# Attention scores: sorted dilated queries, and the low key parts of two heads in one tile

## The chip, the cores and the metric

The kernel runs on one core of one Trainium2 chip. The metric is the device time of one execution in microseconds (us). The profile is one execution, recorded instruction by instruction; its span runs from the first to the last instruction.

## The reference, cut to what matters

The program is a two-layer decoder trunk over 1024 tokens of width 1024. Layer 0 has a gMLP mixer beside an attention mixer, layer 1 a gated linear attention; each is followed by a gated MLP with a short convolution. The change touches layer 0's mixer alone:

```python
B_HEADS, B_HEAD_DIM, B_BLOCK = 8, 64, 128
B_BRANCHES = ((128, 1), (512, 4), (2048, 16))       # window, dilation

qh = rms_norm(heads(q), q_g); kh = rms_norm(heads(k), k_g); vh = heads(vb)
for window, dilation in B_BRANCHES:
    # query t attends to t, t-d, ..., t-window; positions m*d + r form residue
    # subsequences, each a causal band in blocks of 128 (this block and the one before)
    s = jnp.einsum('bhrnic,bhrnjc->bhrnij', qb, kk) * (hd ** -0.5)
    s = jnp.where(valid, s, NEG)
    m = jnp.max(s, -1, keepdims=True); p = jnp.exp(s - m); den = jnp.sum(p, -1)
    o = jnp.einsum('bhrnij,bhrnjc->bhrnic', p, vv) / den[..., None]
    lse = m[..., 0] + jnp.log(den)
wts = jax.nn.softmax(jnp.stack(lses), axis=0)        # over the three branches
o = jnp.einsum('rbhs,rbhsc->bhsc', wts, jnp.stack(outs))
```

## The kernel before

**Precision.** Queries and keys are held as two parts, a high part rounded to fp32r and a low part, the rest (`split`). A score is then (high + low) of the query times (high + low) of the key.

**Work and loops.** The eight heads are done as four pairs (`p` = 0 to 3). `project(p)` goes over eight tiles of 128 tokens (`n`). For each it multiplies the token tile with the pair's weights (`pj`, 24 matmuls of 128x384, in `mm_tok`, L190), normalises (`qn`; row sums on DVE, the power on POOL), puts the parts side by side (`qs`, `ks`), transposes them on TensorE (`tq`, L707; `tk`, L713) and copies them to `qT` and `kT`. It then runs one local block through `unit`. After the eight tiles, `dilated(p)` runs eight blocks of dilation 4; the branch of dilation 16 falls within them and is met by the mask `mboth`. `combine` joins the two sets of outputs.

**The operands of the scores.** `qT` holds, for each head, 64 rows of high part above 64 rows of low part, tokens in order; a dilated block takes its 128 queries as every fourth column. `kT` holds four parts, for each head the high part twice (128 rows) and the low part twice, with the tokens sorted by residue of 4. So one head's score is two matmuls of 128 rows into one PSUM tile `sc`, one with the doubled high key part and one with the doubled low (`scores`, L638).

**After the scores.** DVE adds the mask and takes the row minimum of the negated scores in one instruction (L643), ACT takes the exponential (L644), TensorE transposes the weights (`pP`, L658), DVE or ACT in turn copies them (`pT`, L663 and L661), and TensorE multiplies them with the values (`po`, L666).

**gMLP.** `gmlp` and `u_proj` project to `pv` and `pu`; for each half of the tokens eight products `pm` (L581), one for each group, go to PSUM and DVE adds the bias (L582).

**Order and buffers.** The program is written in its natural order; a scheduler that simulates the engines' time then orders the instructions on each engine. So the projection of pair p+1 stands among the dilated blocks of pair p, and the gMLP among those of the last. Each engine runs its own list in order. PSUM has eight banks, given out by tag: `pt` 2, `sc` 2, `pj` 2, `po` 1, `tq` 1. The `sc` tag serves the scores (one tile for each head of a block) and `pm`.

Of the kernel before, what the change touches and what calls it, by code (L numbers as in the profile page):

```python
# [9 lines left out]
F32 = mybir.dt.float32  # L10
# [45 lines left out]
def trunk(ctx: ExitStack, tc: tile.TileContext, a, out):  # L56
# [452 lines left out]
    def even(gm_open):  # L509
        with ExitStack() as st:  # L510
            pools = {}
            for tag, bufs in (("pt", 2), ("sc", 2), ("pj", 2), ("po", 1), ("tq", 1)):
                pools[tag] = st.enter_context(tc.tile_pool(name="ps_" + tag, bufs=bufs, space=PSUM, reuse_waits="tile"))
            ps = Tagged(pools)
            pq = st.enter_context(tc.tile_pool(name="pq", bufs=1, reuse_waits="tile"))
            par0 = ExitStack()
            pq0 = par0.enter_context(tc.tile_pool(name="pq0", bufs=1, side="right", reuse_waits="tile"))
            with tc.tile_pool(name="nrm", bufs=1, reuse_waits="tile") as pool:
                for n in range(NT):
                    xt = pool.tile([P, D], F32, tag="x", bufs=3, name=f"x0{n}")  # L520
                    Q.dma_start(xt, rows(a["x"], n))
                    if n == 0:
                        Q.dma_start(g0, a["norm_mix_gT"])
                    for g in range(2):
                        pt = ps.tile([P, 4, P], F32, tag="pt", name=f"pt{n}{g}")
                        for j in range(4):
                            k = 2 * j + g
                            T.transpose(pt[:, j, :], xt[:, k * P : (k + 1) * P], ident)
                        split(place(hq[g][n // 4], n), pt)
                    if n == 1:  # L530
                        wq0 = load_qkv(0)
                    h = pool.tile([P, D], F32, tag="h", bufs=2, name=f"h{n}")
                    ssq = small.tile([P, 1], F32, tag="ssq", name=f"ssq{n}")
                    A.activation(h, xt, AF.Square, accum_out=ssq)
                    inv_rms(ssq, 1, D, f"rn{n}", r0[:, n : n + 1])
            with tc.tile_pool(name="at", bufs=2, reuse_waits="tile") as at, \
                    tc.tile_pool(name="av", bufs=1, reuse_waits="tile") as av:
                return attention(ps, at, av, pq, pq0, par0, wq0, gm_open)
# [11 lines left out]
    def gmlp(ps, gm):  # L550
# [14 lines left out]
        def consume(n, pj):  # L565
            gv = gm.tile([P, 512], F32, tag="gv", bufs=2, name=f"gv{n}")
            A.activation(gv, pj, AF.Gelu, scale=r0[:, n : n + 1])
            st = small.tile([P, 6], F32, tag="bn", name=f"bn{n}")
            V.bn_stats(st, gv)
            mv = small.tile([P, 2], F32, tag="mv", name=f"mv{n}")  # L570
            V.bn_aggr(mv, st)
            r = inv_rms(mv[:, 1:2], 1, 1, f"lr{n}")
            V.tensor_scalar(gv, gv, mv[:, 0:1], r, op0=ALU.subtract, op1=ALU.mult)
            V.tensor_mul(gv, gv, lnG)
            half, j = n // 4, n % 4
            V.tensor_add(mx[half][:, j, :], gv, lnB)
            if j == 3:
                for g in range(GROUPS):
                    gc = mx[half][:, :, g * 64 : g * 64 + 64]
                    pm = ps.tile([P, 4, 64], F32, tag="sc", name=f"pm{half}{g}")  # L580
                    T.matmul(pm, ws[:, g, :], gc, start=True, stop=True)  # L581
                    V.tensor_scalar(gc, pm, bs[:, g : g + 1], None, op0=ALU.add)  # L582

# [13 lines left out]
    def attention(ps, at, av, pq, pq0, par0, wq0, gm_open):  # L597
# [33 lines left out]

            return t.rearrange("p s (m r) -> p s r m", r=4)

        def scores(p, name, q, k, W, mask, nm, den, wide):

            sc = ps.tile([P, 256], F32, tag="sc", name="sc" + name)
            for i in range(2):
                T.matmul(sc[:, :W], q, k(i), start=(i == 0), stop=(i == 1))  # L638
            sm = at.tile([P, 256], F32, tag="sm", name="sm" + name, bufs=3)[:, :W]
            o, c, m = wide(sm), sc[:, :W], wide(mask)  # L640
            if len(o.shape) > 2:
                c = c.rearrange("p (r m) -> p r m", r=4)
            V.tensor_tensor_reduce(out=o, in0=c, in1=m, scale=1.0, scalar=3e38, op0=ALU.add, op1=ALU.min, accum_out=nm)  # L643
# [3 lines left out]
        def unit(p, name, i, ot, po, qv, kv, vb, mask, wide=lambda t: t):  # L647
# [2 lines left out]
            nj = len(vb)  # L650
            W = nj * P
            pts = ps.tile([P, 2, nj, P], F32, tag="pt", name="pP" + name)
            for s in range(2):
                sm = scores(p, f"{name}{s}", qv(s), lambda part: kv(s, part), W,
                            mask[:, 2 * P - W :],
                            ot[:, i, 128 + s : 129 + s], ot[:, i, 130 + s : 131 + s], wide)
                for j in range(nj):
                    T.transpose(pts[:, s, j, :], sm[:, j * P : j * P + P], ident)  # L658
# [14 lines left out]
        def project(p, ws=None, then=None):  # L673
# [2 lines left out]
            ws = ws or load_qkv(p)  # L676
            pool = pq if p % 2 else pq0
            qT = pool.tile([P, 2, S], F32R, tag="qT", bufs=1, name=f"qT{p}")
            kT = pool.tile([P, 4, S], F32R, tag="kT", bufs=1, name=f"kT{p}")
            vd = dram.tile([S, P], F32, name=f"vd{p}")  # L680
            vN, os = [], []
            for n in range(NT):
# [14 lines left out]
                A.mul(vN[n], pj[:, 256:384], rn)  # L697
                Q.dma_start(rows(vd, n), vN[n])
                qs = pq.tile([P, 2, P], F32R, tag="qs", bufs=2, name=f"qs{p}{n}")
                ks = pq.tile([P, 4, P], F32R, tag="ks", bufs=2, name=f"ks{p}{n}")  # L700
                split([qs[:, :, :64], qs[:, :, 64:]], heads(qn[:, :P]), hi=G.tensor_copy)
                kk = ks.rearrange("p (h i) (x c) -> p h i x c", i=2, x=2)
                split([kk[:, :, i] for i in range(2)], heads(qn[:, P:])[:, :, None, :].to_broadcast([P, 2, 2, 64]),
                      hi=G.tensor_copy)
                tq = ps.tile([P, 2, P], F32R, tag="tq", name=f"tq{p}{n}")
                for j in range(2):
                    T.transpose(tq[:, j, :], qs[:, j, :], identr)  # L707
                ts_ = slice(n * P, n * P + P)
                A.copy(qT[:, :, ts_], f32(tq))
                four = lambda t: t.rearrange("p s (r m) -> p s r m", r=4)[:, :, :, 32 * n : 32 * n + 32]  # L710
                tk = ps.tile([P, 4, P], F32R, tag="tq", name=f"tk{p}{n}")
                for j in range(4):
                    T.transpose(tk[:, j, :], ks[:, j, :], identr)  # L713
                (V.tensor_copy if n % 2 else A.copy)(four(kT), by4(f32(tk)))

                if n % 4 == 0:
# [1 line left out]
                    os.append(ot)  # L718
                m0 = max(n - 1, 0)
                unit(p, f"{p}n{n}", n % 4, ot, po, lambda s: qT[:, s, ts_],  # L720
                     lambda s, i: kT[:, 2 * s + i, :].rearrange("p (r m) -> p r m", r=4)[:, :, 32 * m0 : 32 * n + 32],
                     vN[m0 : n + 1], mband, lambda t: t.rearrange("p (m r) -> p r m", r=4))
                if n % 4 == 3:
                    A.copy(ot[:, :, :P], po)
# [2 lines left out]
            v4 = av.tile([P, 4, 2, P], F32, tag="v4", name=f"v4{p}", bufs=1)  # L727
            for b in range(2):
                Q.dma_start(v4[:, :, b, :], vd.rearrange("(b m r) c -> b m r c", b=2, r=4)[b])
            return os, qT, kT, v4  # L730

        def dilated(p, qT, kT, v4):

            od = dram.tile([S, 132], F32, name=f"od{p}")
            for g in range(2):
                ot, po = outputs(f"{p}d{g}")
                for i in range(4):
                    r, b = 2 * g + i // 2, i % 2
# [507 lines left out]
```

## Time and profile before

| | |
|---|---|
| Median of three timed executions | 2200.07 us (2199.83 to 2200.43) |
| Span of the profiled execution | 2191.9 us (its own time is not listed apart from the span) |
| Mean granted TensorE clock | 0.998 |
| Busy, share of span | TensorE 98%, weight loads 83%, DVE 70%, ACT 48%, POOL 21% |
| Matmuls | 10508 |
| First and last score matmul (L638) | 37.8 and 353.8 us after the span's start |
| First and last `pm` product (L581) | 357.0 and 394.7 us |

In the profile's rows, PE is TensorE's matmuls and PEld its weight loads; a row of the timeline gives the start, the length, the engine, the line of the code, the tiles written and read, the count of merged instructions, and in brackets the idle time before it with what ended it. A row of groups gives busy time, the mean of one in ns, and the idle time before with its releasers. Matmuls overlap one another, so the length of a merged row holds the tail of its last one.

### The profile page before, as it was taken

How to read it: one execution, taken by the hardware profiler on the slowest of the kernel's cores; microseconds unless marked ns; L12 is line 12 of the kernel's file. 1: busy time of each engine (PE TensorE's matmuls, PEld its weight loads, DVE VectorE, ACT ScalarE, POOL GpSimd, SP SyncE). 2: the span in 40 equal slices, each digit the busy share in tenths (PEclk: the TensorE clock that was granted, in tenths of full speed). 3: DMA queues.
4: the chain of work that ended last, by engine and by line, in shares of the span. 5: the costliest groups of instructions: out<-in, count | busy, mean ns of one | idle time of the engine just before them, and what ended most of it. 6: DMA issues, size and time to landing. Idle time of an engine off the chain costs nothing.

```text
span 2191.9 us, 29865 instructions
## 1 busy us (share of the span) xinstructions
PE 2154.9 (98%) x10508; PEld 1826.3 (83%) x10508; DVE 1532.8 (70%) x2459; ACT 1045.2 (48%) x2006; POOL 468.6 (21%) x487
## 2 busy tenths in 40 slices
PE   8999999999999999999999999999999999999999
PEld 7999987877888888878889787878888888888887
DVE  5566555457888797855577777666887888885554
ACT  6455565246444444444453555534644444454443
POOL 3333320003334252200010011110232424320000
PEclk9999999999999999999999999999999999999999
DMA  4122212565444444575563232378544444557555
GB/s 141 49 77 80 66 48 63 175 242 194 163 158 156 153 158 159 185 287 181 203 234 122 67 98 96 106 234 287 203 150 151 158 166 155 168 177 269 203 195 203
DMA packets 157254, 349.59 MB, mean 159 GB/s; under 512 B 17408, under 2 KB 54272, under 8 KB 156720
## 3 DMA queue, kind: packets, MB, share of 16 engines
q1 hardware_dynamic: 157104, 347.68, 46.9%
q8 instruction: 83, 1.36, 0.3%
q14 instruction: 67, 0.55, 0.1%
HBM read 239.02 MB, written 108.59 MB: 159 GB/s over the span
## 4 chain that ended last, share of the span: by engine, by line
PE 85%; DMA 4%; DVE 4%; ACT 3%; issue 3%; POOL 1%; SPq 0%; ACTq 0%; DVEq 0%; POOLq 0%
PE pgB L290 11%; PE puB L290 11%; PE pgC L290 5%; PE puC L290 5%; PE pj L190 5%; PE pv L190 5%; PE pdB L397 5%; PE pdC L397 5%; PE po L190 5%; PE pdO L397 4%; PE puA L290 3%; PE pgA L290 3%; PE pdP L397 2%; PE pdQ L397 2%; PE pBq L958 2%
## 5 line engine op out<-in xcount | busy, mean ns | idle before, releaser
L101 DVE TENSOR_TENSOR da<-ar,da 128x512 fp32r<-128x512 f32 x154 | 106.2, 690 | 154.3 <-ACT da L100 154.1
L100 ACT CAST da<-ar 128x512 fp32r<-128x512 f32 x154 | 95.9, 623 | 208.3 <-PE pdC L397 89.2
L190 PE MATMUL po<-wo,hq 128*128 128x512 f32 x768 | 184.0, 394 | 1.3 <-ACT hq L100 0.9
L190 PEld LDWEIGHTS po<-wo,hq 128*128 128x128 f32 x768 | 141.7, 188 | 31.2 <-ACT hq L100 1.3
L190 PE MATMUL pj<-wq,hq 128*128 128x384 f32 x768 | 154.4, 347 | 1.5 <-ACT wq L105 1.0
L190 PE MATMUL pv<-wv,hq 128*128 128x512 f32 (+2 forms) x768 | 141.1, 340 | 2.5 <-DVE b L990 1.6
L397 PE MATMUL pdB<-dw,da 128*128 128x512 f32 x528 | 136.2, 391 | 0.8 <-ACT dw L100 0.8
L397 PE MATMUL pdC<-dw,da 128*128 128x512 f32 x528 | 135.8, 390 | 0.0
L190 PEld LDWEIGHTS pj<-wq,hq 128*128 128x128 f32 x768 | 133.3, 191 | 2.7 <-ACT wq L105 1.4
L190 PEld LDWEIGHTS pv<-wv,hq 128*128 128x128 f32 x768 | 118.8, 189 | 17.5 <-DVE b L990 2.1
L397 PEld LDWEIGHTS pdB<-dw,da 128*128 128x128 f32 x528 | 98.7, 188 | 22.1 <-ACT dw L100 1.3
L397 PEld LDWEIGHTS pdC<-dw,da 128*128 128x128 f32 x528 | 99.1, 188 | 20.4
L101 DVE TENSOR_TENSOR dw<-wr,dw 128x512 fp32r<-128x512 f32 x154 | 105.8, 687 | 12.1 <-ACT dw L100 11.8
L256 POOL TENSOR_TENSOR S1g<-rg 128x512 f32<-128x512 f32 x20 | 30.7, 1536 | 381.2 <-DMA wsd<-D 302.0
L140 POOL TENSOR_SCALAR rn<-ssq 128x1 f32<-128x1 f32 x24 | 8.7, 364 | 471.4 <-ACT h L148 245.5
L100 ACT CAST dw<-wr 128x512 fp32r<-128x512 f32 x154 | 95.0, 617 | 15.9 <-DMA wr<-in_w_dn 6.3
L397 PE MATMUL pdO<-dw,da 128*128 128x512 f32 x396 | 102.2, 389 | 0.1
L397 PEld LDWEIGHTS pdO<-dw,da 128*128 128x128 f32 x396 | 74.3, 188 | 15.9 <-DVE dw L101 0.6
L319 DVE SCALAR_TENSOR_TENSOR t<-g,cw,t 128x1022 f32<-128x1022 f32 x44 | 76.6, 1742 | 0.1
L318 DVE SCALAR_TENSOR_TENSOR t<-g,cw,t 128x1023 f32<-128x1023 f32 x44 | 59.3, 1349 | 16.5 <-ACT t L317 16.5
L303 DVE TENSOR_TENSOR g<-g,s1g 128x512 f32<-128x512 f32 x22 | 16.2, 737 | 77.0 <-ACT s1g L302 77.0
L320 ACT ACTIVATE t<-t 128x1024 f32<-128x1024 f32 x44 | 46.7, 1061 | 31.4 <-DVE t L319 31.4
(1069 smaller groups left out, 5407.5 us busy)
## 6 DMA issues: line engine op xcount, KB each, us to landing
ar<-actd SPq DMA_DIRECT2D x70, 512.0 KB, 3.5
rd<-in_w_down SPq DMA_DIRECT2D x44, 512.0 KB, 3.6
wsd<-D SPq DMA_DIRECT2D x88, 256.0 KB, 2.5
rg<-in_w_gate SPq DMA_DIRECT2D x42, 512.0 KB, 3.6
ru<-in_w_up SPq DMA_DIRECT2D x42, 512.0 KB, 4.6
wr<-wsd SPq DMA_DIRECT2D x40, 512.0 KB, 4.6
actd<-t SPq DMA_DIRECT2D x66, 256.0 KB, 2.2
wr<-in_w_dn SPq DMA_DIRECT2D x30, 512.0 KB, 4.8
```

What stands on the lines that cost most here:

```text
L100: (hi or A.copy)(dst[0], src)
L101: (lo or V.tensor_sub)(dst[1], src, f32(dst[0]))
L140: G.tensor_scalar(r, ssq, 1.0 / n, EPS, op0=ALU.mult, op1=ALU.add)
L190: T.matmul(o, L[i], R[jj][:, sl], start=(k == 0 and (ii, jj) == PASSES[0]), stop=(k == nk - 1 and (ii, jj) == PASSES[-1]))
L256: G.tensor_tensor(sums[name], x, y, op=op)
L290: T.matmul(o, L[ii][:, j * P : j * P + P], right[p][:, jj, j, :], skip_group_check=more, start=(not more and j == 0 and (ii, jj) == PASSES ...
L303: V.tensor_add(C22, C22, s1)
L318: V.scalar_tensor_tensor(t[:, 1:], g[:, : S - 1], w(1), t[:, 1:], op0=ALU.mult, op1=ALU.add)
L319: V.scalar_tensor_tensor(t[:, 2:], g[:, : S - 2], w(0), t[:, 2:], op0=ALU.mult, op1=ALU.add)
L320: A.activation(t, t, AF.Silu)
L397: T.matmul(o, L[ii][:, t * P : t * P + P], R[jj], skip_group_check=more, start=start and not more and (ii, jj) == PASSES[0], stop=stop and ...
L958: T.matmul(o, L[ii][:, j * P : j * P + P], right[p][:, jj, j, :], skip_group_check=more, start=(not more and j == 0 and (ii, jj) == PASSES ...
```

## The change

- The low part of the keys is held once for each head: `ks` has three parts, the first head's doubled high part, the second head's doubled high part, and both heads' low parts side by side. `tk` has three transposes instead of four, `kT` three parts.
- `qs` of the second head has its low part above its high part, so that the high query parts of the two heads lie in rows 0 to 63 and 64 to 127, as the low key parts do.
- A head's score is one matmul of 128 rows with the doubled high key part (high and low query times high key), and one of 64 rows (high query times low key). The product of the two low parts is left out.
- Both heads of a block have their scores in one tile of two banks, `[P, 2, 512]`; the tag `sc` has one such buffer instead of two of one bank. The four matmuls are issued first, then each head's mask, minimum and exponential. `pm` takes a tile of the same shape and uses its first bank.
- POOL copies each token tile of `qT` into a new tile `qR` sorted by residue of 4; dilated blocks read their queries there, as 128 columns that lie together.
- The scratch for dynamic DMA is 1024 bytes.

```diff
@@ -577,7 +577,7 @@
             if j == 3:
                 for g in range(GROUPS):
                     gc = mx[half][:, :, g * 64 : g * 64 + 64]
-                    pm = ps.tile([P, 4, 64], F32, tag="sc", name=f"pm{half}{g}")
+                    pm = ps.tile([P, 2, 512], F32, tag="sc", name=f"pm{half}{g}")[:, 0, :256].rearrange("p (a b) -> p a b", a=4)
                     T.matmul(pm, ws[:, g, :], gc, start=True, stop=True)
                     V.tensor_scalar(gc, pm, bs[:, g : g + 1], None, op0=ALU.add)
 
@@ -631,13 +631,11 @@
 
             return t.rearrange("p s (m r) -> p s r m", r=4)
 
-        def scores(p, name, q, k, W, mask, nm, den, wide):
-
-            sc = ps.tile([P, 256], F32, tag="sc", name="sc" + name)
-            for i in range(2):
-                T.matmul(sc[:, :W], q, k(i), start=(i == 0), stop=(i == 1))
+        def scores(name, sc, mask, nm, den, wide):
+
+            W = sc.shape[-1]
             sm = at.tile([P, 256], F32, tag="sm", name="sm" + name, bufs=3)[:, :W]
-            o, c, m = wide(sm), sc[:, :W], wide(mask)
+            o, c, m = wide(sm), sc, wide(mask)
             if len(o.shape) > 2:
                 c = c.rearrange("p (r m) -> p r m", r=4)
             V.tensor_tensor_reduce(out=o, in0=c, in1=m, scale=1.0, scalar=3e38, op0=ALU.add, op1=ALU.min, accum_out=nm)
@@ -650,9 +648,15 @@
             nj = len(vb)
             W = nj * P
             pts = ps.tile([P, 2, nj, P], F32, tag="pt", name="pP" + name)
+            both = ps.tile([P, 2, 512], F32, tag="sc", name=f"sc{name}")
+            scs = [both[:, s, :W] for s in range(2)]
             for s in range(2):
-                sm = scores(p, f"{name}{s}", qv(s), lambda part: kv(s, part), W,
-                            mask[:, 2 * P - W :],
+                T.matmul(scs[s], qv(s), kv(s), start=True, stop=False)
+            for s in range(2):
+                half = slice(64 * s, 64 * s + 64)
+                T.matmul(scs[s], qv(s)[half], kv(2)[half], start=False, stop=True)
+            for s in range(2):
+                sm = scores(f"{name}{s}", scs[s], mask[:, 2 * P - W :],
                             ot[:, i, 128 + s : 129 + s], ot[:, i, 130 + s : 131 + s], wide)
                 for j in range(nj):
                     T.transpose(pts[:, s, j, :], sm[:, j * P : j * P + P], ident)
@@ -676,7 +680,8 @@
             ws = ws or load_qkv(p)
             pool = pq if p % 2 else pq0
             qT = pool.tile([P, 2, S], F32R, tag="qT", bufs=1, name=f"qT{p}")
-            kT = pool.tile([P, 4, S], F32R, tag="kT", bufs=1, name=f"kT{p}")
+            qR = pool.tile([P, 2, S], F32R, tag="qR", bufs=1, name=f"qR{p}")
+            kT = pool.tile([P, 3, S], F32R, tag="kT", bufs=1, name=f"kT{p}")
             vd = dram.tile([S, P], F32, name=f"vd{p}")
             vN, os = [], []
             for n in range(NT):
@@ -697,19 +702,21 @@
                 A.mul(vN[n], pj[:, 256:384], rn)
                 Q.dma_start(rows(vd, n), vN[n])
                 qs = pq.tile([P, 2, P], F32R, tag="qs", bufs=2, name=f"qs{p}{n}")
-                ks = pq.tile([P, 4, P], F32R, tag="ks", bufs=2, name=f"ks{p}{n}")
-                split([qs[:, :, :64], qs[:, :, 64:]], heads(qn[:, :P]), hi=G.tensor_copy)
-                kk = ks.rearrange("p (h i) (x c) -> p h i x c", i=2, x=2)
-                split([kk[:, :, i] for i in range(2)], heads(qn[:, P:])[:, :, None, :].to_broadcast([P, 2, 2, 64]),
-                      hi=G.tensor_copy)
+                ks = pq.tile([P, 3, P], F32R, tag="ks", bufs=2, name=f"ks{p}{n}")
+                q4 = qs.rearrange("p h (x c) -> p (h x) c", c=64)
+                split([q4[:, ::3], q4[:, 1:3]], heads(qn[:, :P]), hi=G.tensor_copy)
+                kh = ks[:, :2].rearrange("p h (x c) -> p h x c", c=64)
+                G.tensor_copy(kh, heads(qn[:, P:])[:, :, None, :].to_broadcast([P, 2, 2, 64]))
+                V.tensor_sub(heads(ks[:, 2]), heads(qn[:, P:]), f32(kh[:, :, 0]))
                 tq = ps.tile([P, 2, P], F32R, tag="tq", name=f"tq{p}{n}")
                 for j in range(2):
                     T.transpose(tq[:, j, :], qs[:, j, :], identr)
                 ts_ = slice(n * P, n * P + P)
                 A.copy(qT[:, :, ts_], f32(tq))
                 four = lambda t: t.rearrange("p s (r m) -> p s r m", r=4)[:, :, :, 32 * n : 32 * n + 32]
-                tk = ps.tile([P, 4, P], F32R, tag="tq", name=f"tk{p}{n}")
-                for j in range(4):
+                G.tensor_copy(four(qR), by4(f32(qT[:, :, ts_])))
+                tk = ps.tile([P, 3, P], F32R, tag="tq", name=f"tk{p}{n}")
+                for j in range(3):
                     T.transpose(tk[:, j, :], ks[:, j, :], identr)
                 (V.tensor_copy if n % 2 else A.copy)(four(kT), by4(f32(tk)))
 
@@ -718,7 +725,7 @@
                     os.append(ot)
                 m0 = max(n - 1, 0)
                 unit(p, f"{p}n{n}", n % 4, ot, po, lambda s: qT[:, s, ts_],
-                     lambda s, i: kT[:, 2 * s + i, :].rearrange("p (r m) -> p r m", r=4)[:, :, 32 * m0 : 32 * n + 32],
+                     lambda s: kT[:, s, :].rearrange("p (r m) -> p r m", r=4)[:, :, 32 * m0 : 32 * n + 32],
                      vN[m0 : n + 1], mband, lambda t: t.rearrange("p (m r) -> p r m", r=4))
                 if n % 4 == 3:
                     A.copy(ot[:, :, :P], po)
@@ -727,9 +734,9 @@
             v4 = av.tile([P, 4, 2, P], F32, tag="v4", name=f"v4{p}", bufs=1)
             for b in range(2):
                 Q.dma_start(v4[:, :, b, :], vd.rearrange("(b m r) c -> b m r c", b=2, r=4)[b])
-            return os, qT, kT, v4
-
-        def dilated(p, qT, kT, v4):
+            return os, qR, kT, v4
+
+        def dilated(p, qR, kT, v4):
 
             od = dram.tile([S, 132], F32, name=f"od{p}")
             for g in range(2):
@@ -737,8 +744,8 @@
                 for i in range(4):
                     r, b = 2 * g + i // 2, i % 2
                     at0 = r * 256
-                    unit(p, f"{p}d{g}{i}", i, ot, po, lambda s: qT[:, s, b * 512 + r : b * 512 + 512 : 4],
-                         lambda s, part: kT[:, 2 * s + part, at0 : at0 + b * P + P],
+                    unit(p, f"{p}d{g}{i}", i, ot, po, lambda s: qR[:, s, at0 + b * P : at0 + b * P + P],
+                         lambda s: kT[:, s, at0 : at0 + b * P + P],
                          [v4[:, r, j, :] for j in range(b + 1)], mboth)
                 A.copy(ot[:, :, :P], po)
                 for b in range(2):
@@ -1235,7 +1242,7 @@
     import concourse.bacc as bacc
     from concourse.bass_utils import run_bass_kernel_spmd
 
-    nc = bacc.Bacc("TRN2", target_bir_lowering=False, num_devices=1)
+    nc = bacc.Bacc("TRN2", target_bir_lowering=False, num_devices=1, dynamic_dma_scratch_size=1024)
     arrays = layouts(inputs)
     aps = {n: nc.dram_tensor("in_" + n, v.shape, F32, kind="ExternalInput").ap() for n, v in arrays.items()}
     out = nc.dram_tensor("out", (S, D), F32, kind="ExternalOutput").ap()
```

(In `even`, the pool of the tag `sc` goes from `("sc", 2)` to `("sc", 1)`.)

More of the change, by code (lines that the diff above doesn't have):

```diff
@@ L511, in even @@
             pools = {}
-            for tag, bufs in (("pt", 2), ("sc", 2), ("pj", 2), ("po", 1), ("tq", 1)):
+            for tag, bufs in (("pt", 2), ("sc", 1), ("pj", 2), ("po", 1), ("tq", 1)):
                 pools[tag] = st.enter_context(tc.tile_pool(name="ps_" + tag, bufs=bufs, space=PSUM, reuse_waits="tile"))
```

## The prediction

> **What bounds the kernel now.** The page comes first: the engines' busy time and the chain that ended last.
>
> ```profile
> span 2191.9 us, 29865 instructions
> PE 2154.9 (98%) x10508; PEld 1826.3 (83%) x10508; DVE 1532.8 (70%) x2459; ACT 1045.2 (48%) x2006; POOL 468.6 (21%) x487
> PE 85%; DMA 4%; DVE 4%; ACT 3%; issue 3%; POOL 1%; SPq 0%; ACTq 0%; DVEq 0%; POOLq 0%
> ```
>
> TensorE carries 85% of the chain. A matmul's modelled time overlaps its neighbour's, so 98% busy only says that gaps are few; what a matmul costs is read from one start to the next. The windows are next: an ordinary attention stretch, the junction of two pairs, and the end of attention.
>
> ```profile
> 150.00:200.00 50.00, 49.79 (x348) 48.84 (x346) 27.09 (x103) 27.09 (x87) 12.48 (x22) 1.00 0.16 45
> 355.00:402.00 47.00, 42.56 (x197) 34.61 (x197) 19.29 (x49) 13.00 (x21) 3.04 (x2) 1.00 0.25 77
> 180.00:193.00 13.00, 12.79 (x105) 12.09 (x105) 9.36 (x36) 10.24 (x35) 2.10 (x4) 1.00 0.31 80
> ```
>
> The columns after the length are PE, PEld, DVE, ACT, POOL, granted clock, DMA share, GB/s. From 150 to 200 TensorE stands for 0.2 of 50 us: attention is bound by TensorE's issue, and what is saved there is saved from the end. At the junction (180 to 193) ACT is busy 10.24 of 13 us, which will matter. Then the tile view of the score matmuls, local (sc1n) and dilated (sc1d):
>
> ```profile
> L638 PEld LDWEIGHTS sc1n<-kT,qT x32: 186/188/216, 114.2 to 152.6; 128*128 128x128 f32 x32
> L638 PE MATMUL sc1n<-kT,qT x32: 277/283/388, 114.3 to 152.7; 128*128 128x256 f32 x28, 128*128 128x128 f32 x4
> L638 PEld LDWEIGHTS sc1d<-kT,qT x32: 307/329/333, 154.6 to 181.8; 128*128 128x128 f32 x32
> L638 PE MATMUL sc1d<-kT,qT x32: 278/399/483, 154.8 to 181.9; 128*128 128x128 f32 x16, 128*128 128x256 f32 x16
> ```
>
> Same shape, but the dilated weight load, whose queries lie four elements apart, takes 329 ns against 188. The timeline says what this costs in issue:
>
> ```profile
> 181.16 1.19 PE L638 MATMUL sc1d<-kT,qT 128*128 128x256 f32 x4
> 182.19 0.29 PE L707 MATMUL tq<-identr,qs 128*128 128x128 f32 x2
> ...
> 183.23 0.30 PEld L638 LDWEIGHTS sc2n<-kT,qT 128*128 128x128 f32 x2
> 183.48 0.14 PEld L658 LDWEIGHTS pP1d<-ident,sm1d 128*128 128x128 f32 x1
> 183.79 0.40 PEld L713 LDWEIGHTS tk<-identr,ks 128*128 128x128 f32 x4
> 184.13 0.42 PEld L658 LDWEIGHTS pP1d<-ident,sm1d 128*128 128x128 f32 x4
> ...
> 213.29 0.64 PE L638 MATMUL sc2n<-kT,qT 128*128 128x256 f32 x4
> 213.76 0.28 PE L707 MATMUL tq<-identr,qs 128*128 128x128 f32 x2
> ...
> 232.39 1.01 PEld L638 LDWEIGHTS sc2d<-kT,qT 128*128 128x128 f32 x4
> 233.34 0.20 PEld L658 LDWEIGHTS pP2d<-ident,sm2d 128*128 128x128 f32 x2
> ```
>
> From the first of a group to the next instruction, over the count: dilated, 256 wide, 1.03/4 = 0.258 us; local, 256 wide, 0.47/4 = 0.118; dilated, 128 wide, 0.95/4 = 0.238; local, 128 wide, 0.25/2 = 0.125; a transpose of ks 0.34/4 = 0.085.
>
> **Part 1: sorted queries (removes).** There are 128 dilated score matmuls (four pairs of 32), half of each width, and all then load contiguous queries: 64 x (0.258 - 0.118) + 64 x (0.238 - 0.125) = 9.0 + 7.2 = 16.2 us less on TensorE.
>
> **Part 2: three key parts instead of four (removes).** 32 transposes go: 32 x 0.085 = 2.7 us. DVE's low part halves and the kT copies shrink by a quarter; both engines have slack outside the junctions, so nothing is counted.
>
> **Part 3: the sorted copy (adds on POOL).**
>
> ```profile
> L100 POOL CAST ks<-qn 128x256 fp32r<-128x256 f32 x29 | 13.1, 450 | 0.9 <-PE tk L713 0.9
> L140 POOL TENSOR_SCALAR rq<-ss 128x4 f32<-128x4 f32 x28 | 8.5, 304 | 86.9 <-DVE ss L691 86.6
> L101 DVE TENSOR_TENSOR ks<-qn,ks 128x256 fp32r<-128x256 f32 x31 | 12.9, 417 | 0.0
> ```
>
> 32 copies of 256 elements at about 0.45 us are 14 us of POOL, which now waits 86.6 us for the row sums alone. The copy waits for ACT's qT; queued behind it in POOL's order are the next token tile's rq and qn, for which DVE and then the transposes wait. The projection runs two PSUM buffers ahead, 24 matmuls each, and covers that: zero. Without that cover, 32 x 0.45 = 14 us. That ks now waits for its high half on POOL alone is the same wait as before. No DMA is added, and none was issued from POOL whose scratch shrinks: zero.
>
> **Part 4: matmuls of 64 rows (changes).** In the changed program's order a block's scores are high, high, low, low, the low ones on rows 0 to 63 and 64 to 127 into two banks. No matmul of the trace has 64 rows, so this is bounded. Below: the two run as one and save 64 x 0.118 = 7.5 us. Above: each change between 128 and 64 rows waits for the matmul before it to end (0.283 modelled, less 0.118 spacing = 0.165) and then for a load that nothing covers (0.118): 0.28 us, at 132 changes in the order (some groups are split) 37 us. I take 0.14 a change, the nearest row being the dilated load, where TensorE likewise waits for a load that isn't covered (0.258 against 0.118): 132 x 0.14 = 18.5; a quarter of the blocks stand where TensorE will wait anyway (part 5), so 13.9; less 7.5 for the pairs: +6.4 us.
>
> [...]
>
> **Part 5: one score tile instead of two (adds a wait).** Before, a head's scores waited for the same head's reduction of the block before; now all four matmuls wait for both reductions.
>
> ```profile
> 182.03 0.42 DVE L643 CUSTOM_DVE_ANT_0 sm1d<-sc1d,mboth 128x256 f32<-128x256 f32 x1 [0.57 <-PE sc1d L638]
> 184.17 0.62 PE L658 MATMUL pP1d<-ident,sm1d 128*128 128x128 f32 x4
> 184.63 0.56 PE L666 MATMUL po1d<-v,pT1d 128*128 128x64 f32 x4
> 189.43 0.63 DVE L643 CUSTOM_DVE_ANT_1 sm2n<-sc2n,mband 128x256 f32<-128x256 f32 x1 [0.30 <-ACT sm2n L644]
> 190.12 0.30 PEld L638 LDWEIGHTS sc2n<-kT,qT 128*128 128x128 f32 x2 [0.44 <-DVE ot2n L643]
> 191.10 1.00 PE L666 MATMUL po2n<-vN,pT2n 128*128 128x64 f32 x8
> ```
>
> The 0.44 at 190.12 is this wait as it exists already. After: the first head's scores are done 0.24 + 0.28 = 0.52 after the block's start, two reductions of 0.63 follow, so the tile is free at 1.8 us (local) or 1.4 (dilated, 0.42 each). Where 13 or more projection matmuls lie between blocks that is covered. At the three junctions, the order puts some eight blocks back to back, with only transposes (0.46 for four) and value matmuls (about 0.45 for four, 0.9 for eight) between: 0.47 + 0.23 + 0.9 = 1.6 and 0.47 + 0.46 + 0.45 = 1.4 against 1.8, twice more 0.1 to 0.2 short: 1 us a junction. ACT takes another: TensorE's 12.79 us there fall by four blocks' 0.5 and some transposes to about 10.5, level with ACT's 10.24, so about 1 us of part 1 comes back as waits for the exponentials. 3 x 2 = +6 us. Ends: 0, and 0.44 for each of the 32 blocks without cover, 14 us.
>
> **Part 6: gMLP's products use the same tile (adds a wait).**
>
> ```profile
> 361.75 0.60 PE L581 MATMUL pm<-mx,ws 128*128 128x256 f32 x2
> 362.39 0.48 DVE L582 TENSOR_SCALAR mx<-pm,bs 128x256 f32<-128x256 f32 x1 [3.58 <-PE pm L581]
> 374.07 0.70 PE L581 MATMUL pm<-mx,ws 128*128 128x256 f32 x2 [1.48 <-DVE mx L582]
> 375.77 1.24 PE L581 MATMUL pm<-mx,ws 128*128 128x256 f32 x4 [1.00 <-DVE mx L582]
> 378.97 4.82 PE L190 MATMUL pu<-wu,hq 128*128 128x512 f32 x20 [1.96 <-ACT ut L592]
> ```
>
> One product's round is 0.64 + 0.48 = 1.12 us (362.39 + 0.48 - 361.75), and two of them now can't overlap. The changed order has seven in a row in the first half, where TensorE lost 1.48 + 1.00 + 1.96 = 4.4 us already: DVE is held there by the combine, and I count no more. The second half ends in three in a row with nothing beside them: two waits of 1.12 less 0.43 own time, +1.5 us. Ends: 0, and 16 x 0.7 = 11.
>
> **Sum.** -16.2 - 2.7 + 6.4 + 6 + 1.5 = -5.0 us on a span of 2191.9. Around the span lie 8.2 us up to the median of 2200.07 (the profiled execution's time is given only as its span), so 2195. All behind attention keeps its instructions; only the second output projection is ordered a little differently.
>
> **Rivals.** 0.2%, 4.4 us, is about what a measurement tells from no change.
>
> First, the row changes are free and the pairs run together: -16.2 - 2.7 - 7.5 + 6 + 1.5 = -18.9, 2181. For it: weight loads here overlap earlier matmuls throughout. Against: none of them changes its rows. [...]
>
> Second, on the other side: a full drain at each change, 0.28 us, and loads that keep the pairs apart: 132 x 0.28 x 0.75 = 27.7, so -18.9 + 27.7 + 7.5 = +16.3, 2216. Its place is either side of the low pair in every block; with pairs that run together, it turns the change slower from 0.19 us a change on (26.4 - 7.5 = 18.9, over 99 exposed). [...]
>
> Third, the single tile binds wherever no projection lies between: 14 instead of 6, +3 us, 2203. For it speak the 0.44 of 190.12 and DVE's other work between the reductions; against, that such blocks are half of all at most.
>
> **How the numbers follow.** The forecast (0.10 to 0.18 us a change, 2190 to 2201) has 0.40: 0.24 faster, 0.14 same, 0.02 slower. First rival 0.22, faster. Second 0.24, slower. Third 0.14: 0.06 same, 0.08 slower. Together 0.46, 0.20, 0.34. Cases of both signs hold much of it, so the range runs from the first rival to just short of the second, 2181 to 2214.
>
> **What the profile after would show.** Dilated loads near 188 ns and 0.12 us apart, 96 tk transposes, 128 matmuls of 64 rows. Right: TensorE's start to start across the low pair is longer by about 0.14 on either side, and the two low matmuls start together. The second rival: about 0.28 there. The third: scores waiting for DVE's L643 in sum well over 6 us. Wrong altogether: dilated loads that stay at 0.24 us apart, or POOL's copy as the wait of the transposes.

## The result, and the profile after

The changed kernel takes 2217.98 us (median of 4 runs, 2215.76 to 2222.19), the kernel before in the same comparison 2199.95 (2198.16 to 2200.43): ratio 1.0084 (95% interval 1.0070 to 1.0098), 18 us slower. The prediction was 2195, range 2181 to 2214. The profiled execution of the changed kernel took 2218.45 us with a span of 2216.4, so 2.05 us lie around a span.

The head of the page after, its clock row and its chain:

```profile
span 2216.4 us, 29798 instructions
PE 2171.8 (98%) x10476; PEld 1820.8 (82%) x10476; DVE 1527.4 (69%) x2459; ACT 1045.1 (47%) x2006; POOL 489.2 (22%) x519
PEclk9999999899999999999999999999999999999999
PE 85%; DVE 5%; DMA 3%; issue 3%; ACT 3%; POOL 1%; SPq 0%; DVEq 0%; ACTq 0%; POOLq 0%
```

The 32 transposes are gone (10476 matmuls for 10508) and POOL has its 32 copies (519 for 487), but TensorE is busy 17 us longer. The windows of the changed kernel say where to look; the column ahead of the DMA share is the granted clock:

```profile
50.00:100.00 50.00, 48.67 (x279) 44.85 (x280) 24.08 (x65) 22.12 (x64) 17.73 (x30) 0.86 0.18 51
150.00:200.00 50.00, 48.03 (x306) 42.34 (x304) 25.64 (x91) 24.35 (x79) 20.91 (x39) 0.93 0.13 38
355.00:402.00 47.00, 41.15 (x179) 31.07 (x178) 19.03 (x56) 18.90 (x33) 3.66 (x4) 0.89 0.24 67
190.00:203.00 13.00, 12.28 (x91) 9.95 (x92) 7.65 (x32) 10.23 (x35) 2.68 (x5) 1.00 0.15 44
```

Before, from 150 to 200 and from 355 to 402 the clock was 1.00; now it is 0.93 and 0.89 (the same windows; the work in them has moved by up to 20 us). Of these windows only the junction (190 to 203), where the prediction put the costs of part 5, stays at 1.00. The mean over the span is 0.989 against 0.998. The tile view of the dilated scores:

```profile
L654 PEld LDWEIGHTS sc1d<-kT,qR x16: 186/189/192, 171.6 to 193.1; 128*128 128x128 f32 x16
L657 PEld LDWEIGHTS sc1d<-kT,qR x16: 182/183/183, 172.5 to 193.5; 64*128 64x128 f32 x16
```

The sorted queries do what they were to do: 189 ns for 329. The timeline of TensorE in the changed kernel, at five places:

```profile
46.59 0.68 PE L654 MATMUL sc0n<-kT,qT 128*128 128x256 f32 x2 [1.52 <-DVE ot0n L641]
49.10 0.76 PE L654 MATMUL sc0n<-kT,qT 128*128 128x256 f32 x2 [0.92 <-DVE ot0n L641]
...
152.91 0.50 PE L654 MATMUL sc1n<-kT,qT 128*128 128x256 f32 x2
153.34 0.39 PE L657 MATMUL sc1n<-kT,qT 64*128 64x256 f32 x2
153.65 0.36 PE L713 MATMUL tq<-identr,qs 128*128 128x128 f32 x2
...
197.56 0.47 PE L654 MATMUL sc2n<-kT,qT 128*128 128x256 f32 x2 [0.16 <-DVE ot2n L641]
...
384.58 0.70 PE L581 MATMUL pm<-mx,ws 128*128 128x256 f32 x2 [0.58 <-DVE mx L582]
387.97 1.15 PE L581 MATMUL pm<-mx,ws 128*128 128x256 f32 x2 [2.69 <-DVE mx L582]
389.69 1.22 PE L581 MATMUL pm<-mx,ws 128*128 128x256 f32 x2 [0.58 <-DVE mx L582]
...
1475.75 1.09 PE L442 MATMUL pc<-ident,cat 128*128 128x128 f32 x8 [2.73 <-DMA cat<-ogd]
```

Three things are to be seen. From 152.91 the two high matmuls, then the two low of 64 rows, then the transposes: 0.43 us to the first low one and 0.31 from it to what follows. The second high matmul starts at 153.126, so the way into the low pair is 0.21 and the way out 0.31, against a spacing of 0.118; the low pair itself starts 3 ns apart (3 or 4 ns in all 62 pairs that run together). Then the waits for the single score tile (46.59, 49.10, 197.56). And at 387.97 the products `pm` go from 0.70 to 1.15 and 1.22 us with the same operands: TensorE runs at half its clock there (0.50 in the window from 388.10). The windows around three such stretches of the changed kernel:

```profile
43.30:46.70 3.40, 1.01 (x7) 0.57 (x7) 3.37 (x13) 1.00 (x4) 1.85 (x3) 1.00 0.00 0
46.70:63.70 17.00, 16.08 (x66) 14.02 (x67) 6.98 (x22) 7.50 (x24) 1.73 (x4) 0.50 0.08 24
384.70:388.10 3.40, 0.71 (x3) 0.31 (x4) 0.96 (x6) 0.22 (x1) 0.00 (x0) 1.00 0.71 159
388.10:398.30 10.20, 8.19 (x16) 4.63 (x17) 8.51 (x23) 2.84 (x4) 2.92 (x2) 0.50 0.09 28
1473.50:1476.90 3.40, 1.15 (x9) 1.13 (x10) 2.68 (x6) 1.81 (x3) 0.00 (x0) 1.00 1.07 383
1476.90:1480.30 3.40, 3.40 (x9) 2.48 (x8) 3.31 (x8) 1.31 (x3) 0.00 (x0) 0.50 1.03 398
```

Each of these three stretches at 0.50 comes behind 3.4 us in which TensorE was little used (1.01, 0.71, 1.15 us; ahead of the other three of this kernel it is 1.40, 2.54 and 2.58), and its length in the trace's record of the clock is a multiple of 3.41: 17.07, 10.24 and 3.41 us. There are six in the changed kernel, 44.4 us in sum, for one of 6.8 us before (at 46.0); a seventh begins 2.2 us ahead of its end. The first follows the wait of 1.52 for the score tile, the fourth the waits of the products for the same tile.

**Where the time went.** For each kernel's profiled execution I took every start to start of TensorE up to the end of attention (the first `pc` transpose) and subtracted the spacing that its form has undisturbed (0.118 for a score matmul, 0.085 for a transpose of ks, and so on); what the 64-row pairs take beyond 4 x 0.118 a block counts as issue. What is left is waiting, or, inside the stretches at 0.50, the cost of the half clock (with the waits inside them). In us:

| up to the first `pc`, then behind it | before | after | difference | forecast |
|---|---|---|---|---|
| issue | 368.6 | 359.4 | -9.2 | -12.5 (parts 1, 2, 4) |
| waits | 26.4 | 40.1 | +13.7 | +7.5 (parts 5, 6) |
| half clock | 3.4 | 20.1 | +16.7 | not in the sum |
| all behind the first `pc` | 1788.8 | 1792.3 | +3.5 | 0 |

The differences add to 24.7, the spans differ by 24.5. The medians differ by 18, because the execution of the kernel before that was profiled was one of its quicker ones: 2191.9 + 2.05 = 2194, at the low end of what it took in the later comparisons (2194.6 to 2206.1).

### The profile page after: what moved, and what is told of

It reads as the page before. It is cut to its first block, busy times and chain, and to the rows that moved or that the text cites. A ratio compares the mean times of both kernels' runs of the same rounds, so it can differ in the third digit from the quotient of the medians.

```text
span 2216.4 us, 29798 instructions
## 1 busy us (share of the span) xinstructions
PE 2171.8 (98%) x10476; PEld 1820.8 (82%) x10476; DVE 1527.4 (69%) x2459; ACT 1045.1 (47%) x2006; POOL 489.2 (22%) x519
## 4 chain that ended last, share of the span: by engine, by line
PE 85%; DVE 5%; DMA 3%; issue 3%; ACT 3%; POOL 1%; SPq 0%; DVEq 0%; ACTq 0%; POOLq 0%
PE puB L290 11%; PE pgB L290 11%; PE po L190 6%; PE pv L190 6%; PE pgC L290 5%; PE puC L290 5%; PE pdB L397 5%; PE pdC L397 5%; PE pj L190 5%; PE pdO L397 4%; PE puA L290 3%; PE pgA L290 3%; PE pdP L397 2%; PE pdQ L397 2%; PE pBq L965 2%
## 5 line engine op out<-in xcount | busy, mean ns | idle before, releaser
L303 DVE TENSOR_TENSOR g<-g,s1g 128x512 f32<-128x512 f32 x22 | 16.2, 738 | 76.9 <-ACT s1g L302 76.9
```

What stands on the lines that cost most here:

```text
L303: V.tensor_add(C22, C22, s1)
```

## The experiments

Three theories stood at the start: the waits of the single tile and of the order high, high, low, low; the changes between 128 and 64 rows; POOL's copy, with the projection behind it. All ratios are to the kernel before on the same chip (medians of 2199.0 to 2200.0 us), with 95% intervals. The column of the order goes by the traces: where a block has two score tiles, the scheduler kept the written order in some blocks only.

| run | sorted queries | rows of the low matmuls | score tiles | order on TensorE | median, us | ratio |
|---|---|---|---|---|---|---|
| before | no | 128 | two | head by head | 2199.4 | |
| e1_sorted_only | yes | 128 | two | head by head | 2190.97 | 0.9968 (0.9954 to 0.9982) |
| e6_both_heads_first | yes | 128 | two | high, high, low, low in 21 of 64 blocks, else mostly head by head | 2199.2 | 0.9998 (0.9989 to 1.0007) |
| e10_after_128_rows | yes | 128 | one | high, high, low, low | 2212.06 | 1.0052 (1.0036 to 1.0068) |
| e2_two_tiles | yes | 64 | two | high, high, low, low in 21 of 64 blocks, else head by head | 2217.65 | 1.0087 (1.0069 to 1.0106) |
| after | yes | 64 | one | high, high, low, low | 2217.98 | 1.0084 (1.0070 to 1.0098) |
| e3_pm_pairs | yes | 64 | one | high, high, low, low | 2218.3 | 1.0086 (1.0069 to 1.0103) |
| e4_one_tile | no | 128 | one | high, high, low, low | 2223.53 | 1.0106 (1.0088 to 1.0125) |
| e7_shared_tile | yes | 128 | one | head by head | 2233.42 | 1.0142 (1.0107 to 1.0176) |
| e8_pm_one_buffer | no | 128 | two | head by head | 2193.95 | 0.9975 (0.9966 to 0.9983) |
| e11_sorted_pm_tq | yes | 128 | two | head by head | 2191.95 | 0.9963 (0.9952 to 0.9975) |

**Sorted queries alone**, on the kernel before, with its four key parts:

```diff
+            qR = pool.tile([P, 2, S], F32R, tag="qR", bufs=1, name=f"qR{p}")
...
+                qT = pq.tile([P, 2, P], F32R, tag="qT", bufs=2, name=f"qT{p}{n}")
+                A.copy(qT, f32(tq))
+                G.tensor_copy(four(qR), by4(f32(qT)))
...
-                    unit(p, f"{p}d{g}{i}", i, ot, po, lambda s: qT[:, s, b * 512 + r : b * 512 + 512 : 4],
+                    unit(p, f"{p}d{g}{i}", i, ot, po, lambda s: qR[:, s, at0 + b * P : at0 + b * P + P],
```

> The kernel before with the sorted queries alone: POOL's copy into qR, contiguous loads in the dilated blocks, four key parts, matmuls of 128 rows, two score tiles of one bank; qT is only a tile per token tile. Theory A (one score tile of two banks and the waits and idle clock that follow it cost the time) and theory B (the changes between 128 and 64 rows cost it) both expect the 16 us of issue to arrive: about 2184, some 16 below the kernel before, and one half-clock stretch of about 7 us near the start, as before. Theory C (POOL's copy delays the projection) expects 2200 or more.

Measured: 2190.97 us, 8 less than before: the quickest kernel of the study, ahead of both given ones (e11_sorted_pm_tq is level with it). Its page, and the tile view of the copy and of the loads:

```profile
PE 2146.9 (98%) x10508; PEld 1815.0 (83%) x10508; DVE 1537.8 (70%) x2459; ACT 1042.5 (48%) x2004; POOL 490.5 (22%) x519
...
L712 POOL CAST qR<-qT x32: 629/650/1099, 29.3 to 297.6; 128x256 fp32r<-128x256 f32 x32
...
L638 PEld LDWEIGHTS sc1d<-kT,qR x32: 186/190/212, 157.8 to 178.0; 128*128 128x128 f32 x32
```

POOL's copies are all there (650 ns each, 20.8 us in sum), and the kernel gains: the third theory falls. The other two expected 2184, and that was missed too: of 16.1 us less issue (368.6 to 352.5) only half reached the end: by the accounting above, waits are 6.8 more than before, half clock 4.7, what lies behind attention 1.2 (3.4 us gained in the profiled executions, where the spans give 3.6).

**Two score tiles again**, on the changed kernel; the 64 rows, the written order and the three key parts stay, `pm` is as before:

```diff
-("sc", 1)
+("sc", 2)
...
-            both = ps.tile([P, 2, 512], F32, tag="sc", name=f"sc{name}")
-            scs = [both[:, s, :W] for s in range(2)]
+            scs = [ps.tile([P, 512], F32, tag="sc", name=f"sc{name}{s}")[:, :W] for s in range(2)]
```

> The changed kernel with two score tiles of one bank for each block instead of one tile of two banks, and gMLP's products in such tiles again; the matmuls of 64 rows stay. Theory A: the waits go, the clock is halved for less than 10 us in sum (44 in the changed kernel), and the time is the issue alone, 16.2 + 2.7 saved against 64 x 0.17 = 11 lost at the row changes: 2190 to 2196. Theory B: not below 2212.

Measured: 2217.65, as the changed kernel. TensorE's chief waits from 40 to 403 us (the waits view: engine, tile and line, for what; us in sum, times, the longest), of the changed kernel first, then of this one:

```profile
PE pm L581 <- DVE mx L582: 5.6, 6, 2.7
PE sc0n L654 <- DVE ot0n L641: 2.4, 2, 1.5
PE tk L720 <- ACT qT L715: 2.3, 4, 0.9
...
PE sc3n L654 <- DVE ot3n L641: 0.6, 2, 0.4
...
PE sc2n L654 <- DVE ot2n L641: 0.5, 2, 0.4
PE sc1n L654 <- DVE ot1n L641: 0.4, 1, 0.4
```

```profile
PE tk L719 <- ACT qT L714: 2.3, 4, 0.9
PE pm L581 <- DVE mx L582: 1.6, 1, 1.6
PE sc0n L653 <- DVE ot0n L641: 1.1, 2, 0.9
```

The tile's waits did shrink, and the time did not. But more than the tile changed. With a tile for each head the scheduler put 43 of the 64 blocks head by head, high, low, high, low:

```profile
201.30 0.36 PE L653 MATMUL sc2n<-kT,qT 128*128 128x256 f32 x1
201.59 0.38 PE L656 MATMUL sc2n<-kT,qT 64*128 64x256 f32 x1
201.90 0.38 PE L653 MATMUL sc2n<-kT,qT 128*128 128x256 f32 x1
202.22 0.38 PE L656 MATMUL sc2n<-kT,qT 64*128 64x256 f32 x1
```

So this run has 218 changes between 128 and 64 rows for the changed kernel's 132, and 19 pairs of low matmuls that run together for its 62. Summed over the starts around the 64-row matmuls of both traces, the time beyond the undisturbed spacing is about 34 us here and 13 in the changed kernel (an estimate). The two tiles saved about as much as the added changes cost, some 21 us; the equal times do not show that the single tile is free.

**Two `pm` products in a tile**, on the changed kernel:

```diff
+                    if g % 2 == 0:
+                        pm2 = ps.tile([P, 2, 512], F32, tag="sc", name=f"pm{half}{g}")
+                    pm = pm2[:, g % 2, :256].rearrange("p (a b) -> p a b", a=4)
```

> The changed kernel with two of gMLP's products in the two banks of one tile; the scores stay in one tile of two banks. Theory A, if gMLP's products are the larger part of it: the 12.7 us from 382 to 395 shrink to about 7 and the half-clock stretch there goes, 2208 to 2211. If the scores' wait is the larger part, or by theory B: 2214 to 2218.

Measured: 2218.3, no difference, but the edit missed its aim: up to 403 us the products' waits are 5.2 us for 5.6. It decides nothing; what `pm` costs is told by the runs with `pm` elsewhere, below.

**One tile and the order alone**, on the kernel before (queries unsorted, 128 rows; `pm` in the tile too):

```diff
+            both = ps.tile([P, 2, 512], F32, tag="sc", name=f"sc{name}")
+            scs = [both[:, s, :W] for s in range(2)]
+            for part in range(2):
+                for s in range(2):
+                    T.matmul(scs[s], qv(s), kv(s, part), start=(part == 0), stop=(part == 1))
```

> The kernel before with the one score tile of two banks alone, for the scores (both high matmuls, then both low) and for gMLP's products; strided queries, four key parts and 128 rows stay. Theory A: slower than before by 15 to 25 us, 2215 to 2225, with half-clock stretches of over 25 us in sum. Theory B: within 5 us of before, 2197 to 2205.

Measured: 2223.53, 24 us more than before, without a single 64-row matmul. In its profile 47.8 us run at half clock; over the kernel before it has 9.3 us more waits, 16.8 more from the half clock, 5.3 more behind attention. This is a larger cost than the whole result. The next runs split it.

**The order**, on e1_sorted_only: the loop of e4_one_tile, with a tile of its own for each head.

> The kernel with sorted queries alone (2191 before), and one thing added: the four score matmuls of a block in the order high, high, low, low, into two tiles of one bank, all of 128 rows. If it is the order that costs (a block's scores can't start until both heads of the last are reduced, and the waits push the clock down): 2203 to 2212, with half-clock stretches of over 25 us. If only the shared tile or only the 64 rows cost: 2188 to 2195.

Measured: 2199.2, 8.2 more than e1_sorted_only. Most of it is the clock (half clock 30.7 us for 17.1 in the profiles). But the order was kept in part only: going by which matmul of a block signals DVE, 21 of the 64 blocks ran as written and at least 39 head by head. One of those, where DVE reduces the first head before the second head's matmuls have begun:

```profile
247.28 0.39 PE L654 MATMUL sc2d<-kT,qR 128*128 128x256 f32 x2
247.72 0.42 DVE L641 CUSTOM_DVE_ANT_0 sm2d<-sc2d,mboth 128x256 f32<-128x256 f32 x1 [1.09 <-PE sc2d L654]
249.39 0.40 PE L654 MATMUL sc2d<-kT,qR 128*128 128x256 f32 x2
```

So 8.2 us is the price of this mixed order, not of the order of the changed kernel.

**The tile without the order**, on e1_sorted_only: both heads in one two-bank tile, head by head, `pm` in the tag `pt`.

```diff
+            both = ps.tile([P, 2, 512], F32, tag="sc", name=f"sc{name}")
...
+                for part in range(2):
+                    T.matmul(both[:, s, :W], qv(s), kv(s, part), start=(part == 0), stop=(part == 1))
```

> The kernel with sorted queries alone, and one thing added: both heads' scores in one tile of two banks, one such tile in all, but head by head (high, low, then high, low); gMLP's products go to the tiles of the transposes, of which there are two, so that they don't meet this tile. If the shared tile costs (it is free only after both reductions): 2203 to 2212. If the order alone costs: 2188 to 2196.

Measured: 2233.42, the slowest, and its six runs spread from 2214.40 to 2241.96. Its waits for the tile:

```profile
PE sc0n L654 <- DVE ot0n L641: 3.5, 4, 2.8
...
PE sc1n L654 <- DVE ot1n L641: 1.8, 5, 0.9
PE sc2n L654 <- DVE ot2n L641: 1.6, 4, 0.9
PE sc3n L654 <- DVE ot3n L641: 1.2, 3, 0.7
PE sc0d L654 <- DVE ot0d L641: 1.1, 3, 0.4
```

The changed kernel has 2.4 in the first of these rows and no listed wait of its dilated blocks. So if one tile is to hold both heads, all its matmuls ahead of the first reduction are better than head by head (2212 in e10_after_128_rows below, where `pm` stands in another tile too). The six runs of this one program go by their clock: 2214.40 at 0.997, 2220.09 at 0.994, 2232.82 at 0.986, 2234.03 at 0.984, 2238.66 at 0.982, 2241.96 at 0.981, or 27.6 us over 0.016, about 1.7 us for 0.001 of mean clock.

**`pm` in the single `tq` buffer**, on the kernel before, and then on e1_sorted_only:

```diff
-                    pm = ps.tile([P, 4, 64], F32, tag="sc", name=f"pm{half}{g}")
+                    pm = ps.tile([P, 4, 64], F32, tag="tq", name=f"pm{half}{g}")
```

> The kernel before, with one buffer for gMLP's products instead of two (they take the tile of the query and key transposes, which stands free by then); the scores stay as they were. If gMLP's share of the one tile is a main part: 2204 to 2210, with a half-clock stretch of 7 to 10 us between 370 and 400. If not: 2198 to 2203.

> Sorted queries alone (2191), and gMLP's products in the tile of the query and key transposes, which gave the kernel before 5 us. If the two add up: 2184 to 2187. If the gain of the products' tile is only another order of the last pair, which the sorted queries change anyway: 2188 to 2193.

Measured: 2193.95, 5.5 less than before; on e1_sorted_only 2191.95, no gain. One buffer for the products costs nothing in itself, and the two gains don't add. Why the first is a gain I have not settled; the order of the last part of attention moves with it.

**The changed kernel with 128 rows** and four key parts; sorted queries, one tile, order and `pm` as changed (the small `qT` tiles of e1_sorted_only and the DMA scratch of before stay):

```diff
-            for s in range(2):
-                T.matmul(scs[s], qv(s), kv(s), start=True, stop=False)
-            for s in range(2):
-                half = slice(64 * s, 64 * s + 64)
-                T.matmul(scs[s], qv(s)[half], kv(2)[half], start=False, stop=True)
+            for part in range(2):
+                for s in range(2):
+                    T.matmul(scs[s], qv(s), kv(s, part), start=(part == 0), stop=(part == 1))
```

> The changed kernel with 128 rows in all score matmuls and four key parts (sorted queries, one score tile of two banks, high, high, low, low, and gMLP's products in the same tile all stay). Against the changed kernel only the 64 rows go. Theory B2 (the 64 rows cost some 18 us, as two tiles with 64 rows at 2218 and two tiles with 128 rows at 2199 suggest): about 2200. Theory A2 (the one tile costs that much by itself in this order, as 2224 for the kernel before with the one tile suggests, and the two don't add up): 2210 to 2218.

Measured: 2212.06. Its trace issues the scores in the written order in 62 of 64 blocks, the changed kernel's in 63, so here the two differ in the rows alone, with the key parts and the two small items named: 6 us. The 18.5 between e2_two_tiles and e6_both_heads_first is no second price of the rows, as e2_two_tiles has 86 more changes than the changed kernel.

Three runs now lead from before to after:

| step | forecast, us | measured, us |
|---|---|---|
| sorted queries (e1_sorted_only) | -16.2 | -8 |
| one tile, the order and `pm` in the tile (e10_after_128_rows against e1_sorted_only) | +7.5 | +21 |
| 64 rows and three key parts (after against e10_after_128_rows) | +3.7 | +6 |

e4_one_tile, on unsorted queries, has 24 for the second step. How the 21 us divide among tile, order and `pm` no run shows, since no run has the order of the changed kernel with two tiles. In the profiled executions, the accounting above gives for this step about +10 us of waits, +8 of half clock and +6 behind attention (my working, with some 2 us of doubt in how waits and half clock divide).

**The clock by itself** (one run): behind the end of the kernel before, bursts of k matmuls of 512 columns, each burst waiting for ACT's copy of the last one's result, between bursts of ten. It adds work, so its time (2435) is not compared.

```diff
+        for k, reps in ((10, 10), (1, 12), (10, 6), (2, 12), (10, 6), (3, 12), (10, 6), (4, 10), (10, 6), (6, 8), (10, 6)):
+            for _ in range(reps):
+                for _ in range(k):
+                    T.matmul(o, identr, r, start=True, stop=True)
+                A.copy(r, o)
```

> The kernel before with a measuring piece behind its end: bursts of 1, 2, 3, 4 and 6 matmuls of 128x512, each burst waiting for ACT's copy of the last, with bursts of 10 between to bring the clock back. [...]

Its timeline, where the bursts of one, of two and of three stand:

```profile
2234.66 0.49 PE L1166 MATMUL dutyo<-dutyr,identr 128*128 128x512 f32 x1 [0.68 <-ACT dutyr L1167]
2235.83 0.50 PE L1166 MATMUL dutyo<-dutyr,identr 128*128 128x512 f32 x1 [0.68 <-ACT dutyr L1167]
2237.00 0.80 PE L1166 MATMUL dutyo<-dutyr,identr 128*128 128x512 f32 x1 [0.68 <-ACT dutyr L1167]
...
2270.61 0.73 PE L1166 MATMUL dutyo<-dutyr,identr 128*128 128x512 f32 x2 [0.73 <-ACT dutyr L1167]
2272.07 0.73 PE L1166 MATMUL dutyo<-dutyr,identr 128*128 128x512 f32 x2 [0.73 <-ACT dutyr L1167]
2273.53 0.83 PE L1166 MATMUL dutyo<-dutyr,identr 128*128 128x512 f32 x2 [0.73 <-ACT dutyr L1167]
2275.09 1.22 PE L1166 MATMUL dutyo<-dutyr,identr 128*128 128x512 f32 x2 [0.73 <-ACT dutyr L1167]
...
2321.31 0.96 PE L1166 MATMUL dutyo<-dutyr,identr 128*128 128x512 f32 x3 [0.73 <-ACT dutyr L1167]
2323.01 0.96 PE L1166 MATMUL dutyo<-dutyr,identr 128*128 128x512 f32 x3 [0.73 <-ACT dutyr L1167]
```

The idle time is 0.68 to 0.73 us in every burst; what differs is the work between. One matmul each 1.17 us: the clock is 0.50 from 2236.5, and still in the first burst of ten behind them (4.64 us from 2248.75; the next, from 2254.12, takes 2.57), some 17 us. Two each 1.46: it is 0.50 from 2274.0 to past 2297, some 24 us. Three each 1.69 keep their 0.96 us, and the bursts of ten run at 1.00 (2205 to 2220). In columns for 3.41 us, the step of the lengths above (512 x k x 3.41 over the period), that is 1490 and 2390 for the halved, 3100 for the threes that keep it. (Counted in the trace, the 3.41 us ahead of the two drops hold 1536 and 3072; three bursts start in each.) The changed kernel fits: each of its six drops comes behind 3.41 us with 512 to 2240 columns, the one of before (46.0) behind 2432, where full stretches hold up to 8192. But the 3072 here stood ahead of a drop, and 1536 without one (before, 377.1), so this is a band and not a sharp line.

## Why the prediction was wrong, step by step

Two steps failed most. The sum priced the single tile, with its order and `pm`, as waits of 7.5 us at full clock, and it cost 21; and it let the 16.2 us of issue arrive in full, and 8 did.

**Part 1 (sorted queries, -16.2)** was right as issue: -16.1 in e1_sorted_only, loads of 190 ns. As time it was half: 8 us. The prediction let TensorE's issue go one for one to the end, from a stretch with 0.2 us of idle time in 50; once TensorE is quicker, it stands earlier before DVE and ACT (6.8 us more of waits in e1_sorted_only).

**Part 2 (three key parts, -2.7)** arrived as 32 transposes less; it was not run alone. **Part 3 (POOL's copy, 0)** was right: the copy takes 0.65 us and not 0.45, and no wait of TensorE's names it; one of 0.55 us, at 44.00, is for an `rq` that stood behind a copy on POOL.

**Part 4 (64 rows, +6.4).** The size of a change was right: 0.21 - 0.118 = 0.09 into the low pair and 0.31 - 0.118 = 0.19 out of it, 0.14 in the mean. That the low pair runs as one, 7.5 us in the sum, no row of before showed; in the changed kernel it does (3 or 4 ns between its starts). A block's four matmuls take 0.64 us for 0.47, so 64 x 0.17 = 11, the uncovered 18.5 - 7.5. What failed is "a quarter of the blocks stand where TensorE will wait anyway": issue fell by 9.2 and not 12.5, which leaves this part 9.6 for 6.4. The second rival's drain of 0.28 a change was not there; its 2216 lies near the result for another reason. What makes a change cost 0.09 and 0.19 us no run shows.

**Part 5 (one score tile, +6)** is the term that was most mis-sized, and its place was wrong. It was worked out for the junctions; the longest waits of the scores came in the first pair (1.52 and 0.92 us at 46.59 and 49.10), and the junction kept its clock. The listed waits for the tile sum to 3.9 us for 0.4 before, under the forecast; but tile, order and `pm` together cost 21 us with 128 rows (e10_after_128_rows against e1_sorted_only), for 7.5 in parts 5 and 6. Of waits alone that step has about 10; what the forecast had at nothing is the half clock and the time behind attention. The order was costed only as the wait for both reductions; its own share stays open.

**Part 6 (`pm`, +1.5)**: its waits rose by 4.4 us (6.9 up to the end of the products, 5.6 of them listed above, for 2.5), and a half-clock stretch of 10.2 us follows the longest. Still no run shows it as a cause of its own: with `pm` back in two tiles its waits fall to 1.6 (e2_two_tiles, where other things changed too), and a single buffer elsewhere costs nothing (e8_pm_one_buffer).

**What the sum lacked is the clock.** +16.7 us in the profiled executions is more than any term. The mean clocks say the same in another way: (0.998 - 0.989) at 1.7 us for 0.001 is 15. The prediction read 1.00 in its windows and took it as given; the 0.97 of the stretch from 50 to 100, and 6.8 us at half clock behind 46.0, stood in the trace of before and were passed over. That waits and thin work lower the clock is shown by the bursts (0.50 with one and with two matmuls between waits of 0.68 to 0.73 us, full with three); that each of the six drops is due to the tile, the order or the 64 rows is not, since a drop is a matter of where the waits meet: the one at 156.0 follows waits for the weights and for ACT's qT, the one at 1476.9 a wait for a transfer, 2.73 us for 1.07 before.

**Around the span** the prediction added 8.2 us; it is 2.05. The rest was the spread of the runs: the profiled one was some 6 us below the median.

## What to carry to other kernels

Here 16.1 us less issue on the bounding engine came to 8 at the end, with 6.8 more of waits and 4.7 more of half clock; cost the waits for a kernel that is already quicker, and try the saving alone first, since the rest of the change took back 27. Look through the granted clock in slices of a few us, not only its mean, before costing an edit that thins the work of TensorE: waits of 0.85 to 2.73 us here were followed by 3.4 to 17 us at half clock. Where a scheduler orders the instructions, look at the order in the trace before reading a run as one thing undone: e2_two_tiles was to give back the second tile alone, and it also broke 43 of the 64 pairs of 64-row matmuls, so that its equal time says nothing of the tile.

## What the runs showed of the hardware

- The half clock needs no long idle time: in e9_duty gaps of 0.73 us, repeated, with two matmuls of 512 columns between, bring it; with three between they don't. As the gaps are as long in both, it was the work between them that decided. The stretches at 0.50 that end inside the spans of before and after last 3.41, 6.83, 10.24 or 17.07 us, whole multiples of 3.41.
- With one matmul a burst the half clock held until the work changed. A matmul then took 0.80 us for 0.49 and the period was 1.47 for 1.17, so still fewer columns came in 3.41 us (1190 for 1490); whether that alone can hold the half clock is not shown, as these bursts are as thin at full clock.
- One program's time moved by 27 us with the clock that it was granted (e7_shared_tile: 2214.40 at 0.997, 2241.96 at 0.981), more than the 18 us that the change cost.
- A change between matmuls of 128 and of 64 rows took 0.09 us more than the spacing of 0.118 on the way in and 0.19 on the way out, and two of 64 rows on different rows start 3 or 4 ns apart (changed kernel, 62 pairs; 152.91 above); head by head (201.30 above) such a low matmul starts 0.29 to 0.32 us behind the high one and the next instruction 0.31 behind it.
